# A hybrid decoder block on one core: the turned blocks of the MLP leave GpSimd's DMA queue for ScalarE's, step by step behind the weight copies

## The chip, the cores and the metric

The kernel runs on one core of a Trainium2 chip, with one launch. The metric is device time in microseconds (us) per execution. The core has five engines with instruction streams of their own: TensorE (PE, with its weight loads as PEld), VectorE (DVE), ScalarE (ACT), GpSimd (POOL) and SyncE (SP). They meet only through semaphores. DMA transfers are issued by an engine's stream and then run beside it.

## The reference

One layer on 272 tokens (16 learned tokens and 256 of the input), width 2048, all in float32:

```python
def reference(x, meta_tokens, ...):
    h = concatenate([meta, x], axis=1)
    h = h + hybrid_mixer(rmsnorm(h, norm_mix_g), w_in, ...)      # attention beside gated linear attention
    h = h + squared_relu_mlp(rmsnorm(h, norm_mlp_g), w_ff1, w_ff2)
    return rmsnorm(h, final_norm_g)[:, N_META:]

def squared_relu_mlp(xn, w1, w2):                                 # 2048 -> 8192 -> 2048
    return jnp.square(jax.nn.relu(xn @ w1)) @ w2
```

The change touches the MLP alone.

## The kernel before

**Products.** Each float32 product is made of a high and a low part. A weight block is loaded in halves of 512 KB by SP into `raw` (5 buffers, L163). ScalarE copies the high part into `w` (L165; L126 in the parts before the MLP), VectorE subtracts and leaves the low part beside it (L166), and `w` has 5 buffers as well. TensorE then multiplies high by high, high by low and low by high (L955, L956, L957).

**The MLP** has the tokens on the partitions where its blocks are wide: `token_rows` goes over 512 columns of weights in four steps (`wide_weights`), each of four k-tiles in two halves, and leaves two banks `pt` of 128 tokens by 512 columns. For the next product the result is wanted the other way about, columns on the partitions. That is what `turn` does: VectorE transposes 32 by 32 squares (L968) into one half of a tile `turn` (tag "o", 2 buffers), four transfers carry its four partition groups to a DRAM tile `there` (2 buffers, L973), and one transfer brings the whole back into the other half (L975).

`hidden` is called 14 times. It makes the squared ReLU (L983, L984, with `u` as its one buffer), turns it, and splits the turned block into `a` for the second product (L224 on ScalarE, a subtract on VectorE). `gathered` sums the second product over groups of columns in `rows`; at the last of the wide groups, four times, it turns `rows` and GpSimd adds the result to the residual `h` (L1012). `spread` runs once, ahead of the first turn: it writes the inverse norms of the 256 tokens to DRAM (`line`, L936) and reads them back to all partitions (`r2b`, L937).

**What sets the order.** `behind` is a list of work with a count; `made` is called once a weight step, after the step's second high copy on ScalarE, counts every entry down, and at zero runs it with the place behind that copy (`issue_after`). `hidden` puts its split at a count of 7. The instruction streams are otherwise placed by a scheduler that goes by its own model of time. After the MLP's wide part, eight blocks of ordinary form follow, the last sums, the final norm and the output (`finish`, L1108 and L1111). The program's closing code has line 1186, its opening code line 1182.

Besides the turns and `spread`, two transfers of the attention part are on GpSimd's queue: `fdram` (L497) and `negc` (L734).

Of the kernel before, what the change touches and what calls it, by code (L numbers as in the profile page):

```python
# [12 lines left out]
ALU = mybir.AluOpType  # L13
# [3 lines left out]
P = 128  # L17
# [3 lines left out]
NT = 256  # L21
# [44 lines left out]
def trunk(ctx: ExitStack, tc: tile.TileContext, hT, w_small, w_all, consts, w_alpha2, out):  # L66
    nc = tc.nc
    serial = [0]

    def nm(s):  # L70
        serial[0] += 1
        return f"{s}_{serial[0]}"
# [11 lines left out]
    def bank(pool, s):  # L84
        return pool.tile([P, 512], F32, tag="bank", name=nm(s))
# [46 lines left out]
    def next_weights(keep_hi=None, meta=False, low=False):  # L132
        c = chunk[0]
        chunk[0] += 1
        parts = []
        for i in range(2):
            hi, lo, step = weight_half(c, i, None if keep_hi is None else keep_hi[:, HK * i : HK * (i + 1), :], meta, low)
            copied = step(0, HK)
            parts.append((hi, lo))
        made(copied)  # L140
        return lambda k: (parts[k // HK][0][:, k % HK, :], parts[k // HK][1][:, k % HK, :])

    behind = []
# [46 lines left out]
    def gemm2(w, x, k0=0, nk=KT, pool=None):  # L190

        ps = bank(pool or pg, "ps")
        for k in range(nk):
            hi, lo = w(k0 + k)
            mac2(ps, hi, lo, x[:, k], k == 0, k == nk - 1)
        issued()
        return ps
# [16 lines left out]
    def total(ps, t=None):  # L214

        b = tmp.tile([P, NT], F32, tag="evb", name=nm("evb"), bufs=1)
        nc.scalar.copy(b, ps[:, NT:512])  # L217
        if t is None:
            t = tmp.tile([P, NT], F32, tag="evt", name=nm("evt"), bufs=4)
        nc.vector.tensor_tensor(t, ps[:, 0:NT], b, op=ALU.add)  # L220
        return t

    def split_to(dst_hi, dst_lo, src):
        nc.scalar.copy(dst_hi, src)  # L224
        nc.vector.tensor_tensor(dst_lo, src, dst_hi.bitcast(F32), op=ALU.subtract)
# [66 lines left out]
    def take(*shape):  # L292
        n = 1
        for d in shape:
            n *= d
        ap = room[:, at_room[0] : at_room[0] + n]
        at_room[0] += n
        if len(shape) == 2:
            ap = ap.rearrange("p (a b) -> p a b", b=shape[1])
        return ap  # L300
# [143 lines left out]
    both = take(NA)  # L444
# [96 lines left out]
    def gla_head(hd, sg, ready=None):  # L541
# [91 lines left out]
        for i in range(4):  # L633
            ps = gemm_all(next_weights(meta=True))
            vT = tmp.tile([P, NA], F32, tag="vT", name=nm("vT"))
            nc.vector.tensor_tensor(vT, ps[:, 0:NA], rb, op=ALU.mult)
            nc.gpsimd.tensor_copy(vg[:, NB * i : NB * (i + 1)], vT[:, 4 * C :])
            later(2 - i % 2 if hd else 1, lambda i=i, vT=vT: turn(i, vT))
# [234 lines left out]
    for j0 in range(0, KT, 2):  # L873
        gates = ahead if j0 == 0 else [gate() for _ in range(4)]
        w = next_weights()
        for j in range(2):
            t = total(gemm2(w, of, k0=8 * j, nk=8))
            nc.vector.tensor_tensor(gates[2 * j], gates[2 * j], t, op=ALU.mult)
        for j in range(2):
            t = total(gemm2(next_weights(), og))  # L880
# [11 lines left out]
    ht = h[:, :, NM:NA]  # L892
# [23 lines left out]
    r2 = gat.tile([P, 2], F32, name="r2", bufs=1)  # L916
    r2b = keep.tile([P, NT], F32, tag="rb", name="r2b")
    parts = gat.tile([P, 2 * NT + 64], F32R, name="parts", bufs=1)[:, 48 : 48 + 2 * NT]
# [14 lines left out]

    def spread():
        line = dram.tile([1, NT], F32, name="line")
        nc.gpsimd.dma_start(line.rearrange("o (t p) -> p (o t)", t=2), r2)  # L936
        nc.gpsimd.dma_start(r2b, line.to_broadcast([P, NT]))  # L937

    def relu2(a, f, ps):
        t = total(ps)  # L940
# [20 lines left out]
        issued()  # L961
        return pts

    def turn(rows):

        both = gat.tile([P, KT * P], F32, tag="o", name=nm("turn"))
        for t, r in enumerate(rows):
            nc.vector.transpose(both[:, 0:1024].rearrange("p (i t j r) -> p t i j r", i=4, t=2, r=32)[:, t],  # L968
                                r().rearrange("p (j i s) -> p i j s", i=4, s=32))
        back = both[:, 1024:]  # L970
        there = dram.tile([P, 1024], F32, tag="there", name=nm("there"), bufs=2)
        for c in range(4):
            nc.gpsimd.dma_start(there.rearrange("(i s) (c e) -> c s i e", i=4, c=4)[c],  # L973
                                both[32 * c : 32 * c + 32, 0:1024].rearrange("s (i e) -> s i e", i=4))
        nc.gpsimd.dma_start(back, there)  # L975
        return back.rearrange("p (c t j r) -> p j t c r", c=4, t=2, r=32)

    def hidden(a, b, pt):

        u = gat.tile([P, 2, 512], F32, tag="u", name=nm("u"), bufs=1)  # L980

        def part(t):
            nc.scalar.activation(u[:, t, :], pt[t], AF.Relu, scale=r2[:, t : t + 1])  # L983
            nc.scalar.activation(u[:, t, :], u[:, t, :], AF.Square)  # L984
            return u[:, t, :]

        back = turn([lambda t=t: part(t) for t in range(2)])

        def parts():
            for t in range(2):  # L990
                hi, lo = (a[:, 4 * b : 4 * b + 4, o, P * t : P * t + P].rearrange("p j (c r) -> p j c r", r=32)
                          for o in range(2))
                split_to(hi, lo, back[:, :, t])

        behind.append([7, parts])

    rows = gat.tile([P, 2, D], F32, name="rows", bufs=1)

    def gathered(g, b, pt):

        rs = [rows[:, t, 512 * b : 512 * b + 512] for t in range(2)]
        for r, ps in zip(rs, pt):
            if g == 0:
                nc.scalar.copy(r, ps)
            else:
                nc.vector.tensor_tensor(r, ps, r, op=ALU.add)
        if g < NG - 2:
            return
        back = turn([lambda r=r: r for r in rs])
        for j in range(4 * b, 4 * b + 4):  # L1010
            r = ht[:, j, :].rearrange("p (t c r) -> p t c r", t=2, r=32)
            nc.gpsimd.tensor_tensor(r, r, back[:, j - 4 * b], op=ALU.add)  # L1012

    def normed(j):
        square_sum(j, acc)
# [5 lines left out]
    for g in range(NG):  # L1021
        a = operand(keep, "a", at=48, tag="s1")
        if g == 1:
            spread()
        for b in range(2 if g == NG - 1 else 4):
            hidden(a, b, *token_rows(x2, 1, norm2 if (g, b) == (0, 0) else None))
        for b0, n in () if g == NG - 1 else ((0, 2), (2, 1), (3, 1)):
            for b, pt in enumerate(token_rows(a, n), b0):
                gathered(g, b, pt)
# [10 lines left out]
    for n in range(NL):  # L1040
        j, ps = KT - NL + n, bank(pg if n < 3 else px, "ps")
# [149 lines left out]
```

## Time and profile before

| what | value |
|---|---|
| time, median of 3 (lowest to highest) | 1534.65 us (1534.22 to 1535.03) |
| profiled execution | 1534.53 us |
| span in its trace | 1532.7 us |
| mean granted clock of TensorE | 0.997 |
| TensorE busy | 1517.7 us, 99% |
| VectorE, ScalarE, GpSimd busy | 65%, 52%, 13% |
| DMA | 311.97 MB, mean 204 GB/s |

The trace's times count from the start of the span; the profiled execution is 1.8 us longer than its span. The rows of the trace name an instruction by its line (L973), its engine, its operation, and what it writes and reads (`there<-turn`); a number behind "x" is a count. A name like POOLq is the engine's sequencer: waits, drains and issues. "[27.27 <-DVE turn L968]" says that the engine idled 27.27 us before, and which work ended that.

### The profile page before, as it was taken

What the parts mean: (1) busy time and instruction counts of PE and PEld (TensorE: products, weight loads), DVE (VectorE), ACT (ScalarE), POOL (GpSimd) and SP (SyncE); (2) the same over time, 40 slices, a digit from 0 to 9 for tenths busy, and PEclk for the clock granted to TensorE, in tenths of its full rate; (3) what the DMA queues carried; (4) which work ended last, traced back from release to release, by engine and by line L of the source; (5) the groups of instructions that cost most, each with busy time, mean ns of one, the idle gap of its engine ahead of it and who ended that gap; (6) DMA issues with size and microseconds to landing.
All of it is one profiled execution on the core that took longest, in us unless ns stands there. A gap on an engine that the chain in (4) does not pass through costs nothing.

```text
span 1532.7 us, 23498 instructions
## 1 busy us (share of the span) xinstructions
PE 1517.7 (99%) x8982; PEld 1367.8 (89%) x8982; DVE 992.4 (65%) x1421; ACT 799.0 (52%) x1203; POOL 198.3 (13%) x322
## 2 busy tenths in 40 slices
PE   9999999999999999999999999999999999999996
PEld 8999999999999999999998888888888888888996
DVE  7898858586666666666787555445555556657655
ACT  7666454555555544445666455444543554345563
POOL 6012010111100000000011110001100110430022
PEclk9999999999999999999999999999999999999998
DMA  9545555565555665566566787668866777877561
GB/s 327 169 153 173 185 160 191 159 214 168 165 169 188 196 199 196 195 200 198 189 208 195 206 268 235 201 194 258 255 199 201 226 254 225 285 235 241 196 201 65
DMA packets 172593, 311.97 MB, mean 204 GB/s; under 512 B 10601, under 2 KB 124785, under 8 KB 172353
## 3 DMA queue, kind: packets, MB, share of 16 engines
q1 hardware_dynamic: 165744, 289.62, 59.0%
q0 software_dynamic: 6304, 20.14, 4.3%
q8 instruction: 70, 1.15, 0.3%
q10 hardware_dynamic: 432, 0.72, 0.1%
q14 instruction: 43, 0.34, 0.1%
HBM read 298.89 MB, written 11.54 MB: 203 GB/s over the span
## 4 chain that ended last, share of the span: by engine, by line
PE 95%; DVE 2%; ACT 1%; issue 1%; DMA 0%; POOL 0%; SPq 0%; POOLq 0%; DVEq 0%; ACTq 0%
PE ps L179 27%; PE ps L180 14%; PE pt L957 12%; PE pt L955 12%; PE pt L956 12%; PE psa L184 4%; PE psa L188 4%; PE psa L186 4%; PE ps L397 1%; PE ps L1060 1%; PE ps L399 1%; DVE w L127 1%; PE ps L1044 1%; PE pa L595 0%; DMA raw<-w_all_dram 0%
## 5 line engine op out<-in xcount | busy, mean ns | idle before, releaser
L127 DVE TENSOR_TENSOR w<-raw,w 128x1024 fp32r<-128x1024 f32 x314 | 389.5, 1241 | 161.1 <-ACT w L126 158.2
L166 DVE TENSOR_TENSOR w<-raw,w 128x1024 fp32r<-128x1024 f32 x208 | 255.6, 1229 | 240.1 <-ACT w L165 239.9
L126 ACT CAST w<-raw 128x1024 fp32r<-128x1024 f32 x314 | 329.2, 1049 | 138.8 <-PE ps L180 78.4
L179 PE MATMUL ps<-x,w 128*128 128x512 f32 x1056 | 355.8, 382 | 0.0
L165 ACT CAST w<-raw 128x1024 fp32r<-128x1024 f32 x208 | 217.5, 1046 | 261.7 <-PE pt L957 258.3
L180 PE MATMUL ps<-x,w 128*128 128x256 f32 x1056 | 289.6, 274 | 0.0
L179 PEld LDWEIGHTS ps<-x,w 128*128 128x128 f32 x1056 | 198.2, 188 | 33.7
L180 PEld LDWEIGHTS ps<-x,w 128*128 128x128 f32 x1056 | 198.3, 188 | 0.0
L184 PE MATMUL psa<-x,w 128*128 128x272 f32 x640 | 181.8, 285 | 0.0
L188 PE MATMUL psa<-x,w 128*128 128x272 f32 x640 | 179.7, 282 | 0.0
L186 PE MATMUL psa<-x,w 128*128 128x272 f32 x624 | 176.0, 282 | 0.0
L957 PE MATMUL pt<-w,x 128*128 128x512 f32 x448 | 170.3, 380 | 0.0
L955 PE MATMUL pt<-w,x 128*128 128x512 f32 x448 | 170.3, 380 | 0.0
L956 PE MATMUL pt<-w,x 128*128 128x512 f32 x448 | 170.2, 380 | 0.0
L957 PE MATMUL pt<-w,a 128*128 128x512 f32 x384 | 145.9, 380 | 0.0
L955 PE MATMUL pt<-w,a 128*128 128x512 f32 x384 | 145.9, 380 | 0.0
L956 PE MATMUL pt<-w,a 128*128 128x512 f32 x384 | 145.9, 380 | 0.0
L184 PEld LDWEIGHTS psa<-x,w 128*128 128x128 f32 x640 | 120.2, 188 | 0.2
L188 PEld LDWEIGHTS psa<-x,w 128*128 128x128 f32 x640 | 120.2, 188 | 0.1
L186 PEld LDWEIGHTS psa<-x,w 128*128 128x128 f32 x624 | 117.4, 188 | 0.0
L217 ACT COPY evb<-ps 128x256 f32<-128x256 f32 x104 | 38.6, 371 | 126.4 <-PE ps L180 126.4
L957 PEld LDWEIGHTS pt<-w,x 128*128 128x128 f32 x448 | 84.1, 188 | 14.5
(324 smaller groups left out, 2335.1 us busy)
## 6 DMA issues: line engine op xcount, KB each, us to landing
raw<-w_all_dram SPq DMA_DIRECT2D x537, 512.0 KB, 4.5
there<-turn POOLq DMA_DIRECT2D x72, 128.0 KB, 4.7
turn<-there POOLq DMA_DIRECT2D x18, 512.0 KB, 4.8
raw<-w_all_dram SPq DMA_DIRECT2D x8, 384.0 KB, 6.6
h<-hT_dram SPq DMA_DIRECT2D x8, 275.0 KB, 7.0
negc<-fdram POOLq DMA_DIRECT2D x1, 1088.0 KB, 8.7
out_dram<-o SPq DMA_DIRECT2D x2, 512.0 KB, 2.7
raw<-w_all_dram SPq DMA_DIRECT2D x2, 256.0 KB, 3.6
```

Source lines behind the costliest of these rows:

```text
L126: copied = nc.scalar.copy(hi[:, k, :], r).ins
L127: nc.vector.tensor_tensor(lo[:, k, :], r, hi[:, k, :].bitcast(F32), op=ALU.subtract)
L165: copied = nc.scalar.copy(hi, r).ins
L166: nc.vector.tensor_tensor(lo, r, hi.bitcast(F32), op=ALU.subtract)
L179: nc.tensor.matmul(steps(ps), hi, steps(row(x)), start=first, stop=False)
L180: nc.tensor.matmul(steps(ps[:, 0:NT]), lo, steps(x[:, 0, :]), start=False, stop=last)
L184: nc.tensor.matmul(steps(ps[:, X_LO]), hi, steps(x_lo[:, k]), start=first, stop=False, skip_group_check=True)
L186: nc.tensor.matmul(steps(ps[:, 0:NA]), lo, steps(x_hi[:, k]), start=False, stop=last and hi is None, skip_group_check=True)
L188: nc.tensor.matmul(steps(ps[:, 0:NA]), hi, steps(x_hi[:, k]), start=False, stop=last, skip_group_check=True)
L955: nc.tensor.matmul(steps(ps), xh, steps(hi), start=(k == 0), stop=False)
L956: nc.tensor.matmul(steps(ps), xh, steps(lo), start=False, stop=False)
L957: nc.tensor.matmul(steps(ps), xl, steps(hi), start=False, stop=(k == KT - 1))
```

## The change

The four transfers to `there` and the one back go from GpSimd's queue to ScalarE's. They are no longer issued when the transposes are made: the four stand behind the copy of the 5th following weight step, the one back behind the 6th, and what uses the turned block (the split in `hidden`, GpSimd's adds in `gathered`) behind the 7th. `spread`'s two transfers go to SP's queue.

```diff
     def spread():
         line = dram.tile([1, NT], F32, name="line")
-        nc.gpsimd.dma_start(line.rearrange("o (t p) -> p (o t)", t=2), r2)
-        nc.gpsimd.dma_start(r2b, line.to_broadcast([P, NT]))
+        nc.sync.dma_start(line.rearrange("o (t p) -> p (o t)", t=2), r2)
+        nc.sync.dma_start(r2b, line.to_broadcast([P, NT]))
...
-    def turn(rows):
+    def turn(rows, then):
...
-        for c in range(4):
-            nc.gpsimd.dma_start(there.rearrange("(i s) (c e) -> c s i e", i=4, c=4)[c],
-                                both[32 * c : 32 * c + 32, 0:1024].rearrange("s (i e) -> s i e", i=4))
-        nc.gpsimd.dma_start(back, there)
-        return back.rearrange("p (c t j r) -> p j t c r", c=4, t=2, r=32)
+
+        def away():
+            for c in range(4):
+                nc.scalar.dma_start(there.rearrange("(i s) (c e) -> c s i e", i=4, c=4)[c],
+                                    both[32 * c : 32 * c + 32, 0:1024].rearrange("s (i e) -> s i e", i=4))
+
+        behind.append([5, away])
+        behind.append([6, lambda: nc.scalar.dma_start(back, there)])
+        behind.append([7, lambda: then(back.rearrange("p (c t j r) -> p j t c r", c=4, t=2, r=32))])
...
-        back = turn([lambda t=t: part(t) for t in range(2)])
-
-        def parts():
+        def parts(back):
...
-        behind.append([7, parts])
+        turn([lambda t=t: part(t) for t in range(2)], parts)
...
-        back = turn([lambda r=r: r for r in rs])
-        for j in range(4 * b, 4 * b + 4):
-            r = ht[:, j, :].rearrange("p (t c r) -> p t c r", t=2, r=32)
-            nc.gpsimd.tensor_tensor(r, r, back[:, j - 4 * b], op=ALU.add)
+
+        def add(back):
+            for j in range(4 * b, 4 * b + 4):
+                r = ht[:, j, :].rearrange("p (t c r) -> p t c r", t=2, r=32)
+                nc.gpsimd.tensor_tensor(r, r, back[:, j - 4 * b], op=ALU.add)
+
+        turn([lambda r=r: r for r in rs], add)
```

How the streams move. TensorE's is the same in both. The first place is ScalarE's stream behind the first turned block, from the copies of the fifth following weight step on. Before, no transfer stands in it:

```order
L165 CAST w_9740<-raw_9739 128x1024
L165 CAST w_9745<-raw_9744 128x1024
L165 CAST w_9774<-raw_9773 128x1024
L165 CAST w_9779<-raw_9778 128x1024
L983 ACTIVATE u_9723<-pt_9581,r_9245 128x512
L983 ACTIVATE u_9723<-pt_9582,r_9245 128x512
L165 CAST w_9808<-raw_9807 128x1024
L984 ACTIVATE u_9723<-u_9723 128x512 x2
L165 CAST w_9813<-raw_9812 128x1024
L224 CAST a_9252<-turn_9568 128x4x128 x2
```

After the change the same place holds the four transfers, and two copies on, the one back:

```order
L165 CAST w_9730<-raw_9729 128x1024
L165 CAST w_9735<-raw_9734 128x1024
L975 DMA there_9570<-turn_9563 32x4x256 x4
L165 CAST w_9768<-raw_9767 128x1024
L165 CAST w_9773<-raw_9772 128x1024
L979 DMA turn_9563<-there_9570 128x1024
L987 ACTIVATE u_9718<-pt_9571,r_9245 128x512
L987 ACTIVATE u_9718<-pt_9572,r_9245 128x512
L165 CAST w_9803<-raw_9802 128x1024
L988 ACTIVATE u_9718<-u_9718 128x512 x2
L165 CAST w_9808<-raw_9807 128x1024
L224 CAST a_9252<-turn_9563 128x4x128 x2
```

The copies, the activations and the split keep their order; the transfers are put between them, and the one back waits in ScalarE's stream for the four to land.

The second place is GpSimd's stream at the gathered blocks. Before, it issues the transfers of two blocks and then adds:

```order
L973 DMA there_12555<-turn_12552 32x4x256 x4
L973 DMA there_12570<-turn_12567 32x4x256 x4
L975 DMA turn_12552<-there_12555 128x1024
L975 DMA turn_12567<-there_12570 128x1024
L1012 TENSOR_TENSOR h<-h,turn_12552 128x256 x4
L1012 TENSOR_TENSOR h<-h,turn_12567 128x256 x4
```

After the change only the adds are left, of all four gathered blocks one behind the other:

```order
L1015 TENSOR_TENSOR h<-h,turn_12552 128x256 x4
L1015 TENSOR_TENSOR h<-h,turn_12558 128x256 x4
L1015 TENSOR_TENSOR h<-h,turn_12702 128x256 x4
L1015 TENSOR_TENSOR h<-h,turn_12864 128x256 x4
L901 TENSOR_TENSOR acc_9251<-acc_9251,hsq_13712 128x256
```

Every transfer of the MLP has left this stream. The third place is SP's stream where `spread` stands now, between the weight loads (`raw`):

```order
L163 DMA raw_9533<-w_all_dram 128x4x256
L936 DMA line<-r_9245 128x2x1
L163 DMA raw_9573<-w_all_dram 128x4x256
L937 DMA r2b<-line 128x256
L163 DMA raw_9578<-w_all_dram 128x4x256
```

One weight load goes between the two, and the load behind `r2b` is issued after `line` has landed.

## The prediction

> **What bounds the kernel now.** I read the page's busy shares first, then busy time by stage, then the waits, then the end of the chain.
>
> ```profile
> PE 1517.7 (99%) x8982; PEld 1367.8 (89%) x8982; DVE 992.4 (65%) x1421; ACT 799.0 (52%) x1203; POOL 198.3 (13%) x322
> ```
>
> Stretches of the program (columns: TensorE busy, its weight loads, VectorE, ScalarE, GpSimd, granted clock, DMA share, GB/s). The middle one is the MLP, where all the turns lie:
>
> ```profile
> core 0: us, PE busy (x) PEld busy (x) DVE busy (x) ACT busy (x) POOL busy (x), PEclk, DMA share, GB/s
> 0.00:860.00 860.00, 857.84 (x5734) 796.68 (x5735) 612.23 (x1006) 467.01 (x794) 112.60 (x196) 1.00 0.59 191
> 860.00:1430.00 570.00, 570.00 (x2652) 488.27 (x2651) 321.57 (x323) 279.84 (x321) 66.01 (x107) 1.00 0.74 233
> 1430.00:1533.00 103.00, 89.89 (x600) 82.89 (x598) 58.61 (x93) 52.13 (x89) 19.67 (x19) 0.96 0.46 149
> ```
>
> TensorE is busy in 570.00 of the 570.00 us that hold the turns, at a granted clock of 1.00. So a shorter turn buys nothing there. The change can lose time in this stage, by making TensorE wait, and can gain none. What is not TensorE lies in the last stretch: 103.00 − 89.89 = 13.1 us. The chain of waits ends with these two rows (start, duration, engine):
>
> ```profile
> 1517.06 2.35 POOL o L1108 x2
> 1519.41 3.12 issue
> ```
>
> What follows 1522.5 is the closing code, line 1186: a drain on each engine, then a barrier (duration in ns min/median/max, then first and last start):
>
> ```profile
> L1186 POOLq DRAIN  x3: 40/102/9402, 1522.5 to 1532.4; - x3
> L1186 DVEq DRAIN  x2: 19/936/1853, 1522.3 to 1532.2; - x2
> L1186 ACTq DRAIN  x2: 8/79/150, 1524.6 to 1532.2; - x2
> ```
>
> GpSimd's drain of 9402 ns began at 1522.5 and ended at 1531.9. Its last arithmetic was over long before, and so was everybody else's. GpSimd's last products, the transfers of the output, and SP's drains behind the waits for these transfers:
>
> ```profile
> 1522.56 1.59 POOL L1108 TENSOR_TENSOR o<-h,r_half 128x256 f32<-128x256 f32 x2 [3.15 <-DVE r_half L1093]
> L1111 SPq DMA_DIRECT2D out_dram<-o x4: 332/338/348, 1518.0 to 1524.2; - x4
> L1111 ACTq DMA_DIRECT2D out_dram<-o x3: 338/374/381, 1522.8 to 1524.2; - x3
> DMA to landing us min/median/max: 1.8/2.6/3.1
> L1186 SPq DRAIN  x2: 7/7/7, 1527.4 to 1527.5; - x2
> ```
>
> GpSimd's arithmetic ends at 1522.56 + 1.59 = 1524.15, the last output lands by about 1524.2 + 3.1 = 1527.3, and SP is done at 1527.5. From 1527.5 to 1531.9 nothing runs but GpSimd's drain, and the barrier behind it takes 1532.7 − 1531.93 = 0.77 us. VectorE's drain of 1853 ns from 1522.3 ends with its last product and is no such case. So **4.4 us of the span are GpSimd's drain alone**.
>
> **The change part by part.** GpSimd's queue loses the second and third of these kinds of transfer (count, KB each, median us to landing), and the two in `spread`:
>
> ```profile
> raw<-w_all_dram SPq DMA_DIRECT2D x537, 512.0 KB, 4.5
> there<-turn POOLq DMA_DIRECT2D x72, 128.0 KB, 4.7
> turn<-there POOLq DMA_DIRECT2D x18, 512.0 KB, 4.8
> ```
>
> It keeps two, `fdram` and `negc`: of 94 transfers 92 go.
>
> *The drain.* Two drains of GpSimd with no transfer issued since the one before take 102 and 40 ns (the row above), and the one at the kernel's start takes 186:
>
> ```profile
> L1182 POOLq DRAIN  x1: 186/186/186, 0.4 to 0.4; - x1
> ```
>
> The long one, which has all 94 transfers behind it, lasts 7.8 us beyond GpSimd's last product. SP, with 537 large loads behind it, drained in 7 ns, so the price belongs to GpSimd's queue. No trace here shows whether it grows with the number of transfers. Bounds: 0.2 us (no work on the queue) and 7.8 us (a fixed price once the queue was used). In proportion, 2 × 7.8 / 94 = 0.17 us, an estimate. I take the low end: of four drains in this run the three without transfers are short, and 2 of 94 is nearer to none. Then GpSimd is done at about 1524.4, SP at 1527.5 ends last, and the span ends at 1527.5 + 0.77 = 1528.3: **−4.4 us**. Any drain below 3.3 us gives the same, since SP covers it.
>
> *Four more issues and one back issue on ScalarE, per turn.* TensorE's pace, the copies that follow it, and the copies' and the subtracts' groups in the MLP (busy us, mean ns of one | idle before, and what ended it):
>
> ```profile
> 876.85 0.38 PE L955 MATMUL pt<-w,x 128*128 128x512 f32 x1
> 877.07 0.38 PE L956 MATMUL pt<-w,x 128*128 128x512 f32 x1
> 877.29 0.38 PE L957 MATMUL pt<-w,x 128*128 128x512 f32 x1
> 1296.81 1.05 ACT L165 CAST w<-raw 128x1024 fp32r<-128x1024 f32 x1 [1.59 <-PE pt L957]
> 1299.45 1.05 ACT L165 CAST w<-raw 128x1024 fp32r<-128x1024 f32 x1 [1.59 <-PE pt L957]
> L165 ACT CAST w<-raw 128x1024 fp32r<-128x1024 f32 x196 | 204.9, 1046 | 250.2 <-PE pt L957 247.7 <-DMA raw<-w_all_dram 2.5
> L166 DVE TENSOR_TENSOR w<-raw,w 128x1024 fp32r<-128x1024 f32 x197 | 242.2, 1229 | 234.9 <-ACT w L165 234.9
> ```
>
> A matmul starts every 0.22 us, a half block holds 12, so a buffer of `w` falls free every 2.64 us; ScalarE copies 1.05 of that and idles 1.59. Five buffers: when a copy starts, four others are ahead, 4 × 2.64 = 10.56 us; less the copy and VectorE's 1.23 us, **8.28 us of delay reach TensorE as nothing**. The four `there` issues take 4 × 0.37 = 1.5 us (ACT issues above), inside one idle of 1.59. The back transfer is queued one weight step later, and ScalarE must wait there for the four to land. With L from issue to landing, in us after the copy it hangs on: the step's two copies end at 2.64 and 5.28, the back issue goes at max(5.28, 1.5 + L). At L = 4.7 that is 6.2, 0.9 later than the queue alone would have it. Behind it stand Relu (two of 0.69), the next copies, the squares (two of 0.63) and two casts of `a` (0.61):
>
> ```profile
> L983 ACT ACTIVATE u<-pt,r 128x512 f32<-128x512 f32 x28 | 18.9, 689 | 13.1 <-PE pt L957 13.1
> L984 ACT ACTIVATE u<-u 128x512 f32<-128x512 f32 x28 | 16.1, 625 | 0.0
> L224 ACT CAST a<-turn 128x512 fp32r<-128x512 f32 x28 | 15.9, 614 | 0.0
> ```
>
> The copy behind Relu then starts at 6.2 + 0.37 + 1.35 = 7.9 in place of 6.87, 1.0 late. The casts of `a` need the back transfer: 6.2 + 4.8 = 11.0, and the copy behind them starts at about 12.3 in place of 12.15. Each later copy wins back up to 1.59. Both delays lie inside 8.28: **0 us**. Were the cover gone they would cost 1.0 and 0.15 us a turn. In general the copy is 2L − 9.5 late (both transfers taken alike); delay carries into the next turn from L = 7.1 (2L − 14.3 a turn) and a single turn stalls TensorE from 8.9. Where two blocks are gathered at once, eight transfers share `there`'s two tiles, and VectorE's subtracts queue behind a transpose that waits for GpSimd's adds: there the stall begins at L = 6.4 and is 2L − 12.8.
>
> L is not in the trace for ScalarE's queue. The bounds are the output writes above (1.8) and the slowest `there` (7.7):
>
> ```profile
> L973 POOL DMA_DIRECT2D there<-turn x72: 551/551/587, 869.6 to 1395.2; - x72
> DMA to landing us min/median/max: 2.3/4.7/7.7
> L975 POOL DMA_DIRECT2D turn<-there x18: 552/557/573, 878.9 to 1400.9; - x18
> ```
>
> I take 4.7: same bytes, same stage, same traffic of weights. SP's larger loads, at 4.5, stand on the same side.
>
> *GpSimd.* It loses 72 × 0.55 = 40 us of issuing and its place in the turn; its adds to `h` move behind the seventh weight step, and the residual that reads them comes after 1430. With TensorE busy throughout the stage, nothing there waited for it: 0.
>
> *`spread` on SP.* The weight loads queue behind `r2b`, which waits for `line`:
>
> ```profile
> 858.60 0.79 POOL L936 DMA_DIRECT2D line<-r  x1 [16.16 <-DVE r L268]
> 869.00 0.56 POOL L937 DMA_DIRECT2D r2b<-line  x1 [9.62 <-DMA line<-r]
> 872.63 1.04 ACT L165 CAST w<-raw 128x1024 fp32r<-128x1024 f32 x1 [2.45 <-DMA raw<-w_all_dram]
> L163 SPq DMA_DIRECT2D raw<-w_all_dram x4: 368/368/368, 860.9 to 868.8; - x4
> DMA to landing us min/median/max: 9.5/10.0/11.6
> L163 SPq DMA_DIRECT2D raw<-w_all_dram x4: 368/368/368, 871.5 to 879.4; - x4
> DMA to landing us min/median/max: 6.9/7.1/9.2
> ```
>
> The last rows are SP's loads between 860 and 870, then 870 and 880, one every 2.64 us. `line` lands at 858.6 + 0.8 + 9.6 = 869.0; the load behind `r2b` leaves at about 869.4 in place of 863.5, 5.9 late, and the later ones catch up. A load leaves when the copy and subtract before it have freed its buffer, and of five buffers its own copy comes some 5 × 2.64 − 2.3 = 10.9 us later; landing in 7 to 10, it makes that copy 2 to 5 us late (estimates). The slack of 8.28 is already short by the 2.45 us of the third row; 5 + 2.45 = 7.5 still fits, barely. Bounds 0 and 3 us; I take 0.
>
> **Sum.** Against the profiled execution (1534.53 us, span 1532.7): −4.4 + 0 + 0 = 1530.1. The median shown is 0.1 above that execution: **1530.2 us**. Runs of before lie within 0.4 of their median, and small stalls may take 0.6, so this case alone spans 1529.4 to 1531.2. A change of 0.2%, 3.1 us, is about what a measurement of this kernel can tell.
>
> **Rivals.**
>
> *The drain is a fixed price.* Two transfers are still on GpSimd, and the trace has no drain behind only a few. Against it: nothing of the transfers can be outstanding, the last of them (1400.9) over 100 us old; for it: a flat clean-up need not count. Then the span stays, 1534.6. So does a drain that shrinks by less than 3.1 us. The Trainium skill ("DMA: Bandwidth & Descriptors", section "Issuing engines are not separate DMA queues") speaks for this one: transfers run on the same 16 engines whoever issues them, and only issue time on the sequencer is saved. By that rule the change is worth nothing; in the trace the issues on GpSimd are indeed off the path, but the 7.8 us drain is a cost that it does not count. Together 0.38.
>
> *ScalarE's queue is held by its own waits: slower.* Place: the back issue of a turn, and above all the gathered blocks. From L = 6.4 the gathered blocks stall TensorE, from 7.1 single turns carry delay over. At L = 7.7: 2 × 7.7 − 12.8 = 2.6 us; and with 5.9 late in a first turn and 1.1 more in each further one, the fourth of a group is 9.2 late, 0.9 over the slack, in three groups: 5.4 us in all: 1534.6 + 5.4 = 1540.0, or 1535.6 with the shorter drain. At L = 10 a turn costs 5.7 us, some 80 in all. For it: 7.7 did occur. Against it: it is the slowest of 72, and writes by ScalarE's and SP's queues, those of the output, landed in 3.1 at most. The Trainium skill ("Perfetto Trace Analysis", section "DMA Instruction — HWDGE (DVE, Sync)") warns that the completion of a write to HBM can take surprisingly long; the writes to `there` are of that kind, and the median of 4.7 us against 2.6 for the output writes agrees in direction only. A stall of 3 us at `spread` belongs here only where the drain stays (1537.6; 1533.2 with the short drain). Together 0.15.
>
> **How the numbers follow.** Short drain, no stall: 0.47. Drain unchanged or nearly, or its gain eaten by a stall: 0.38. Slower: 0.15. The range from 1529.4 to 1536.5 holds the first case, the second, and stalls of up to 2 us on top of it; it leaves out the held queue's 1540 and more, some 0.13, and a few in 100 below. Faster 0.47, same 0.38, slower 0.15.
>
> **What would show it.** Right: GpSimd's last drain ends before SP's, near 1525, the span ends at about 1528.3, TensorE is still busy throughout the MLP, and ScalarE's copies wait for TensorE as now. Wrong: the same 9.4 us drain with two transfers behind it (fixed price); gaps in TensorE at the gathered blocks or next to 880, or `there` on ScalarE's queue landing after 7 us (held queue).

## The result, and the profile after

The changed kernel takes 1531.08 us (median of 13 runs, 1530.41 to 1532.01), the kernel before 1534.67 in the same comparison: a ratio of 0.9977, 95% interval 0.9968 to 0.9985. That is 3.6 us faster, against 4.4 forecast; the time is 0.9 us above the forecast and inside its range.

The closing drains of the changed kernel, line 1191 now (duration in ns min/median/max, first and last start):

```profile
L1191 POOLq DRAIN  x3: 93/188/1881, 1523.2 to 1529.7; - x3
L1191 SPq DRAIN  x3: 7/7/7, 1528.8 to 1529.1; - x3
L1191 SPq EVENT_SEMAPHORE  x9: 17/28/28, 1528.4 to 1530.0; - x9
```

GpSimd's last products in its timeline:

```profile
1523.26 1.59 POOL L1113 TENSOR_TENSOR o<-h,r_half 128x256 f32<-128x256 f32 x2 [3.15 <-DVE r_half L1098]
```

The drain of 9402 ns has become one of 1881. As before, it starts with the last products and cannot end before them: 1.881 − 1.59 = 0.29 us beyond them, where it was 9.402 − 1.59 = 7.81. Now SP, waiting for the output, is last.

TensorE's stage is untouched (busy of TensorE, its loads, VectorE, ScalarE, GpSimd, then clock, DMA share, GB/s), and so are ScalarE's copies, except for a few waits:

```profile
860.00:1430.00 570.00, 570.00 (x2652) 488.34 (x2651) 321.64 (x323) 279.22 (x321) 16.40 (x16) 1.00 0.72 232
```

```profile
ACT w L165 <- PE pt L957: 238.5, 158, 2.5
...
ACT w L165 <- DMA there<-turn: 9.8, 3, 4.2
ACT w L165 <- DMA raw<-w_all_dram: 7.7, 4, 3.4
```

The waits (us in total, times, longest) show ScalarE's weight copies held by landings for 17.5 us in all, and TensorE is still busy 570.00 of 570.00. ScalarE's splits and activations wait another 7.7 us for the turned block's transfers. The transfers that moved (lines 975 and 979 are `there` and the one back, on ScalarE's queue; line 936 is `line` on SP's):

```profile
L975 ACTq DMA_DIRECT2D there<-turn x72: 309/458/1543, 877.1 to 1405.0; - x72
DMA to landing us min/median/max: 3.7/4.3/6.3
L979 ACTq DMA_DIRECT2D turn<-there x18: 344/344/418, 884.7 to 1410.7; - x18
DMA to landing us min/median/max: 3.9/5.1/6.8
L936 SPq DMA_DIRECT2D line<-r x1: 500/500/500, 858.7 to 858.7; - x1
DMA to landing us min/median/max: 11.0/11.0/11.0
```

They land about when they did on GpSimd's queue: 4.3 after 4.7, and 5.1 after 4.8.

### The profile page after: what moved, and what is told of

Read it like the earlier page. It is cut to its first block, busy times and chain, and to the rows that moved or that the text cites. A ratio compares the mean times of both kernels' runs of the same rounds, so it can differ in the third digit from the quotient of the medians.

```text
span 1530.1 us, 23462 instructions
## 1 busy us (share of the span) xinstructions
PE 1518.0 (99%) x8982; PEld 1368.0 (89%) x8982; DVE 992.8 (65%) x1421; ACT 798.2 (52%) x1203; POOL 148.5 (10%) x230
## 3 DMA queue, kind: packets, MB, share of 16 engines
q8 instruction: 70, 1.15, 0.3%
## 4 chain that ended last, share of the span: by engine, by line
PE 94%; DVE 2%; ACT 2%; issue 1%; DMA 1%; POOL 0%; POOLq 0%; DVEq 0%; ACTq 0%
PE ps L179 26%; PE ps L180 13%; PE pt L957 12%; PE pt L956 12%; PE pt L955 12%; PE psa L184 4%; PE psa L188 4%; PE psa L186 4%; PE ps L397 1%; DVE w L127 1%; DMA raw<-w_all_dram 1%; PE ps L399 1%; PE ps L1065 1%; ACT w L126 1%; PE pa L595 0%
```

## Experiments

Theory: GpSimd's drain pays for every transfer that it issued since its last drain, some 83 ns each, and the change is worth what of that lay beyond the end of everything else. Rivals: it pays by bytes or packets; it is a fixed price; it belongs to the end of the program and not to the transfers. Apart from that: does any of the moved waits cost TensorE, and why is the gain 0.8 us short?

### The price of the drain

**e1: the number without the bytes.** The changed kernel with 90 tiny transfers added:

```diff
+        for i in range(5):
+            nc.gpsimd.dma_start(spot[len(turns) - 1, i : i + 1, :], unit[0:1, 0:64].bitcast(F32))
```

> The changed kernel with 90 transfers of 256 bytes added on GpSimd's queue, 5 to each turn, so that 92 transfers stand there again with hardly any bytes. If the closing drain pays by the number of transfers (7.8 us / 94 = 83 ns each): 92 x 83 ns = 7.6 us beyond GpSimd's last product, and the time is back at about 1534.5. If it pays by bytes or packets (20.14 MB, 6304 packets before): about 0.5 us, covered by SP, 1531.1. TensorE's stages unchanged in both.

```profile
L1198 POOLq DRAIN  x3: 40/102/9242, 1531.7 to 1541.5; - x3
```

```profile
1531.77 1.60 POOL L1120 TENSOR_TENSOR o<-h,r_half 128x256 f32<-128x256 f32 x2 [3.15 <-DVE r_half L1105]
```

```profile
q0 software_dynamic: 3056, 1.15, 0.3%
```

```profile
L971 POOL DMA_DIRECT2D spot<-unit x90: 484/484/553, 759.6 to 827.5; - x90
```

(Drains, GpSimd's last products, the page's line on GpSimd's queue with packets, MB and share, and the added transfers.) With 92 transfers and 1.15 MB the drain is back: 9.242 − 1.60 = 7.64 us, where 7.6 was expected by number and 0.5 by bytes. The added transfers need nothing from the turns, and the scheduler put all 90 between 760 and 828 us, not beside the turns: they were issued some 700 us before the closing drain, and it pays for them all the same. The time missed: 1544.95, with runs from 1534.24 to 1555.52. In the profiled run (1543.49) GpSimd's last products start 9.2 us later than before the change, so that excess arose while TensorE worked ("what was not expected" below). From there to the end of the span it is 10.0 us, as it was before (10.1).

**e2 and e3: part of the transfers.** In e2 only the transfers back are on GpSimd's queue, in e3 the first 9 of the 18 turns:

```diff
-        behind.append([6, lambda: nc.scalar.dma_start(back, there)])
+        behind.append([6, lambda: nc.gpsimd.dma_start(back, there)])
```

```diff
+        eng = nc.gpsimd if len(turns) <= 9 else nc.scalar
...
-                nc.scalar.dma_start(there.rearrange(
+                eng.dma_start(there.rearrange(
```

> The changed kernel with the 18 transfers back from DRAM alone on GpSimd's queue, 20 transfers in all with 10.5 of the 20.1 MB. By number: 20 x 83 ns = 1.7 us of drain, covered by SP's waits for the output, time as the changed kernel, 1531.1. By bytes: 4.1 us of drain, about 0.5 us past SP, 1531.6.

> The changed kernel with the first 9 of the 18 turns on GpSimd's queue, 47 transfers. By number or by bytes: 3.9 to 4.2 us of drain, some 0.3 us past SP: 1531.4. A price that does not depend on how much (all or nothing): 7.8 us, 1534.6.

Drains and last products, e2:

```profile
L1191 POOLq DRAIN  x3: 40/93/3351, 1522.1 to 1527.5; - x3
```

```profile
1522.11 1.59 POOL L1113 TENSOR_TENSOR o<-h,r_half 128x256 f32<-128x256 f32 x2 [3.15 <-DVE r_half L1098]
```

and e3:

```profile
L1196 POOLq DRAIN  x3: 40/93/5563, 1521.7 to 1527.7; - x3
```

```profile
1521.68 1.59 POOL L1118 TENSOR_TENSOR o<-h,r_half 128x256 f32<-128x256 f32 x2 [3.15 <-DVE r_half L1103]
```

1.76 us with 20 transfers, 3.97 with 47. Both carry 10.56 MB, so bytes are out: by them the two would be alike. Packets are out too: they are 2768 in e2, 3200 in e3 and 3056 in e1, which does not follow the drain. In e3 the last of the 47 was issued at 1210.0, over 300 us before the closing drain; that drain ends at 1521.7 + 5.56 = 1527.3, some 0.6 us after SP's first closing drain (1526.6). The times are 1529.85 (ratio 0.997, 0.9958 to 0.9982) and 1530.32 (0.9972, 0.996 to 0.9984), 1.1 to 1.3 us below what was expected of each; the part on the missing 0.8 us comes back to that.

**e4 and e9: the same 94 transfers, cleared up early.** The kernel before with one line more, behind the last turn:

```diff
     for f in range(8, KT):
+        if f == 12:
+            tc.keep_in_program_order(nc.gpsimd.drain())
         relu2(a, f, gemm2(next_weights(low=True), x2))
```

> The kernel before with one more drain of GpSimd behind its last turn, while TensorE still has about 100 us of work; the 94 transfers stay on GpSimd's queue. If the drain clears up what transfers left behind, the early one takes the 7.8 us unseen, the closing one is short (0.2 us past the last product), and the time falls to about that of the changed kernel, 1531.1. If the long drain belongs to the end of the program, the closing one stays at 7.8 us and the time at 1534.6.

> The kernel before with the early drain once more, in more rounds. It measured 1530.3 against 1531.1 of the changed kernel. If clearing up early is worth all that the moved transfers are worth, and the changed kernel's slightly longer tail is its own, it is again at 1530.0 to 1530.6; if the difference was scatter, at 1531.0.

The added drain, the closing ones and the last products of e4:

```profile
L1032 POOLq DRAIN  x1: 8794/8794/8794, 1401.4 to 1401.4; - x1
L1188 POOLq DRAIN  x3: 34/93/1689, 1522.7 to 1528.1; - x3
```

```profile
1522.68 1.59 POOL L1110 TENSOR_TENSOR o<-h,r_half 128x256 f32<-128x256 f32 x2 [3.15 <-DVE r_half L1095]
```

The early drain takes 8.79 us at 1401, beside TensorE's work, and leaves 0.10 for the end. The time is 1530.29 in e4 and 1530.31 in e9 (ratios 0.9973, intervals 0.9962 to 0.9983 and 0.9963 to 0.9983): the whole gain, with not one transfer moved. The drain is paid once for what came since the one before; it does not belong to the end.

**e7 and e10: under the cover.** e7 also moves `fdram` and `negc` to SP, e10 is e2 with the early drain of e4.

> The changed kernel with the last two transfers of GpSimd (fdram, negc) on SP's queue as well, so none is left. By number of transfers: the drain falls by another 0.17 us under SP's cover, time as the changed kernel, 1530.2 to 1531.1. If any use of GpSimd's queue has a price at the end, below 1530.

> The changed kernel with the 18 transfers back on GpSimd's queue and the early drain. The closing drain falls from 1.75 to 0.1 us past the last product, both under SP's waits for the output: no change against that kernel without the drain, 1529.6 to 1530.2. If the drain were still on the path at 1.75 us, 1.5 less.

e7's drain is 1691 ns, 0.10 beyond 1.59 of products. e10's closing drain is 1789 ns, 0.20 beyond, where 0.1 was expected: its early drain stands at 1389.5, and one transfer back follows at 1411.9. The times are 1530.80 (0.9976, 0.9967 to 0.9986) and 1530.20 (0.9973, 0.9962 to 0.9984, against 1529.85 without the early drain). Below some 3 us the drain costs nothing that these runs can tell: e2's 1.76 us and e10's 0.20 both end before SP's wait for the output.

In one row: beyond the last product, 0.10, 0.20, 0.29, 0.45, 1.76, 3.97, 7.64 and 7.81 us with 0, 1, 2, 4, 20, 47, 92 and 94 transfers since the last drain (the one with 4 is e6, below: a drain of 2052 ns over 1.60 of products). **0.10 us + 82 ns per transfer** gives 0.10, 0.18, 0.26, 0.43, 1.74, 3.95, 7.64 and 7.81.

These are closing drains, over 100 us behind the last transfer. The early drains are less regular. Those of e9 and e10:

```profile
L1033 POOLq DRAIN  x1: 10507/10507/10507, 1402.1 to 1402.1; - x1
L1037 POOLq DRAIN  x1: 6132/6132/6132, 1389.5 to 1389.5; - x1
```

Their records start with the issue of a transfer back, some 0.56 us. For the 94 and 19 transfers issued by then the rule gives 7.8 and 1.7 us; e4's early drain, 8.79 us, has 94 too. So a drain right behind a transfer that has not landed took longer than the rule, by 0.4 to 3.9 us beyond the issue, and what fills that time stays open.

### The waits that moved

**e6: `spread` back on GpSimd's queue.**

```diff
-        nc.sync.dma_start(line.rearrange("o (t p) -> p (o t)", t=2), r2)
-        nc.sync.dma_start(r2b, line.to_broadcast([P, NT]))
+        nc.gpsimd.dma_start(line.rearrange("o (t p) -> p (o t)", t=2), r2)
+        nc.gpsimd.dma_start(r2b, line.to_broadcast([P, NT]))
```

> The changed kernel with the two transfers of spread back on GpSimd's queue: 4 transfers, drain 0.3 us past the last product. If spread on SP costs nothing, as forecast, the time is that of the changed kernel, 1530.2 to 1531.1; if the loads held behind it cost TensorE up to 3 us, this kernel is that much faster.

1530.53 (0.9974, 0.9965 to 0.9984), half a microsecond under the changed kernel and inside the scatter of both. SP's held loads cost no more than that.

**e12: the counts of 5 and 6 taken away.**

```diff
-        behind.append([5, away])
-        behind.append([6, lambda: nc.scalar.dma_start(back, there)])
+        away()
+        nc.scalar.dma_start(back, there)
```

> The changed kernel without the counts of 5 and 6: the transfers are queued on ScalarE as soon as the scheduler sees them ready, some four weight steps earlier, the same number of issues and waits per turn. By the slack of 8.28 us nothing reaches TensorE: 1530.2 to 1531.1. If the counts are what keeps ScalarE from waiting, for the transposes above all, several us slower, 1535 or more.

1531.06 (0.9977, 0.9968 to 0.9986): the same as with the counts. Where in the five weight steps ScalarE issues the transfers does not matter to the time, though its weight copies now wait 26.2 us for the landings of `there`, in place of 9.8.

**e11 and e8: more waits in ScalarE's queue.** One and two transfers more per turn, each waiting for the one ahead:

```diff
-        behind.append([5, away])
-        behind.append([6, lambda: nc.scalar.dma_start(back, there)])
+        behind.append([5, lambda: (away(), nc.scalar.dma_start(back, there), nc.scalar.dma_start(again, back))])
```

(e8 has `nc.scalar.dma_start(more, again)` behind these. Both also queue the transfer back at the count of 5; e12 shows that its place alone costs nothing.)

> The changed kernel with one more wait per turn in ScalarE's queue: the copy of the turned block to DRAM, issued once the transfer back has landed. Two more waits cost 26 us, where the landing of there had risen to 5.5 median and 9.3 at most. With one more and landings near 5 the copies run 6 to 7 us late, inside 8.28: 1531 to 1534. If any further wait breaks the cover, 1540 to 1550.

> The changed kernel with two more waits in ScalarE's queue per turn: behind the transfer back, ScalarE also issues a copy of the turned block to DRAM and a copy of that copy, each once the one before has landed. By the forecast's slack: back issued at 5.8, the third transfer at 11.3, the fourth at 16.1, so the copies of the next weights run up to 6.9 us late; 8.28 covers that, TensorE stays busy at single turns, and only the two blocks gathered at once may cost up to 5 us: 1531 to 1536. If ScalarE's waits reach TensorE, each of 18 turns pays two waits of some 5 us less the idle of 1.59: well over 1580.

Both missed, upwards. e11 takes 1538.85 (nine runs, 1530.47 to 1540.89; a tenth took 1558.98 and is left out; ratio 1.002, 1.0008 to 1.0033), e8 1557.08 (1.0138, 1.0114 to 1.0162). What TensorE waited for (us in total, times, longest) in e8, the longest first:

```profile
PE pt L955 <- ACT a L224: 4.8, 2, 3.8
PE ps L180 <- DVE w L127: 2.7, 4, 0.8
PE pt L957 <- DVE a L225: 2.1, 3, 1.0
```

and in e11:

```profile
PE pt L957 <- DVE a L225: 2.0, 3, 0.8
```

The first thing to be late is not a weight but `a`, the turned block itself: the first gathered product of a group needs the block that the fourth `hidden` turned, and that split stands behind the held queue. In e11 TensorE waited for no weight in the MLP, so the slack of 8.28 us, worked out for weights, was not used up there. The rest of e11's and e8's loss is told below.

### The missing 0.8 us

**e5: the changed kernel once more.**

> The changed kernel once more. It measured 1531.1, 0.9 above the forecast. If the 0.7 us wait of TensorE near 1497 and the longer barrier of its trace belong to that one execution, they are gone here and the time is 1530.2 to 1530.5; if they belong to the kernel, they recur and the time is 1531.1.

1531.05 (0.9977, 0.9968 to 0.9986): it recurs. In the first trace of the changed kernel TensorE had one wait that the kernel before does not have; it ended at 1500.3, not near 1497 (us in total, times, longest):

```profile
PE ps L1049 <- DVE h L906: 0.7, 1, 0.7
```

That wait does not recur: in e5 GpSimd's last products start at 1522.69, 0.13 later than before the change. What recurs is the tail:

```profile
L1192 SPq EVENT_SEMAPHORE  x9: 17/28/28, 1527.8 to 1529.4; - x9
L1192 POOLq DRAIN  x3: 93/188/1882, 1522.7 to 1529.0; - x3
L1192 SPq DRAIN  x3: 7/7/7, 1528.2 to 1528.5; - x3
L1192 POOLq EVENT_SEMAPHORE_RANGE_CLEAR  x1: 142/142/142, 1528.6 to 1528.6; - x1
```

```profile
L1117 ACTq DMA_DIRECT2D out_dram<-o x3: 344/374/392, 1523.0 to 1524.3; - x3
DMA to landing us min/median/max: 1.8/2.6/3.4
```

The slowest output transfer lands after 3.4 us in place of 3.1, and all of SP's closing waits run one behind the other after it: SP is done at 1528.2, 0.7 later than the forecast's 1527.5. From there to the end of the span (1529.5) it is 1.3 us in place of 0.77, since GpSimd's last drain (1529.0) stands 0.3 us behind its clearing of semaphores (1528.6 + 0.14) and takes 0.19, where it took 0.04 before. Together 1.2: −4.4 + 1.2 = −3.2, the span of e5 against that of before.

From the start of GpSimd's last products to the end of the span the forecast had 1528.3 − 1522.56 = 5.7 us. It is 6.8 in both traces of the changed kernel, and 5.7 in e2, e4, e9 and e10, the faster ones, where that gap is not there. The gap is not the whole account: e12 is without it (6.3 us there) and takes as long as the changed kernel. What opens the gap and delays the landing was not found.

## Why the prediction was right

- **TensorE's stage can lose and not gain:** so it was, 570.00 of 570.00 before and after.
- **The drain is the gain:** right, in mechanism and size. But no trace showed then whether the drain shrinks with the number of transfers; the prediction chose the low end of its bounds, and e1 to e4 showed only afterwards that the choice was sound. The estimate of 83 ns per transfer, made in proportion from one row, was 82 by eight rows; 0.2 us were forecast for what remains, 0.29 came.
- **What ends last then:** right that it is SP behind the output, but mis-sized: SP at 1527.5 and a barrier of 0.77 were taken over from the trace of before. They measured 1528.2 and 1.3 in e5. That is the whole distance between −4.4 and −3.2 us.
- **ScalarE's queue:** 0 was right, L was 4.3 and 5.1 where 4.7 and 4.8 were taken; an issue took 0.46 where 0.37 was taken. But the cover named for it was not the only one: the list of who waits left out TensorE's wait for `a`, and e11 and e8 show that this comes first. The rival's prices (2L − 12.8, carry from L = 7.1) rested on the weights alone, and no run here bears them out. Its comparison of 4.7 us for `there` with 2.6 for the output says nothing of writes to DRAM, since both are such writes.
- **`spread` on SP:** 0, as forecast. `line` took 11.0 us, and ScalarE's waits for weight loads rose from 2.5 to 7.7 us, all of it inside the slack.
- **The fixed price:** ruled out by e2 and e3. The Trainium skill's rule beside it ("DMA: Bandwidth & Descriptors", "Issuing engines are not separate DMA queues") holds for the transfers themselves, whose landings hardly changed (4.3 us after 4.7, 5.1 after 4.8); but it counts only the time to issue as what another issuer can save, and here 82 ns more per transfer fell due at GpSimd's drain.

## What to carry to other kernels

Read the last microseconds of the trace. Where GpSimd's closing drain ends after every other engine is done, count the transfers that GpSimd issued: here each cost 82 ns, however small and however long landed. One early drain, in a stretch where nothing waited for GpSimd, took that away without moving a transfer. When a wait is put into a queue, list every reader of what stands behind it, the result that the wait serves included.

## What was not expected of the hardware

TensorE's pace changed for hundreds of microseconds, in e11 from a short wait on. Its timeline there:

```profile
935.27 0.38 PE L955 MATMUL pt<-w,a 128*128 128x512 f32 x1
935.49 0.39 PE L956 MATMUL pt<-w,a 128*128 128x512 f32 x1
936.35 0.50 PE L957 MATMUL pt<-w,a 128*128 128x512 f32 x1 [0.47 <-DVE a L225]
...
1000.35 0.38 PE L955 MATMUL pt<-w,a 128*128 128x512 f32 x1
1000.58 0.39 PE L956 MATMUL pt<-w,a 128*128 128x512 f32 x1
1000.80 0.38 PE L957 MATMUL pt<-w,a 128*128 128x512 f32 x1
1001.02 0.39 PE L955 MATMUL pt<-w,a 128*128 128x512 f32 x1
```

Before the wait a matmul starts every 0.220 us, after it every 0.2235, with the granted clock at 1.00 in both (TensorE's busy time and matmuls in 30 us, clock, DMA share, GB/s):

```profile
900.00:930.00 30.00, 30.00 (x139) 1.00 0.87 286
...
960.00:990.00 30.00, 30.00 (x136) 1.00 0.68 221
1200.00:1230.00 30.00, 30.00 (x136) 1.00 0.70 224
```

At 136 in place of 138 per 30 us from 936 to about 1390, some 6.6 us are lost (an estimate), beside waits of 2.0: about the distance of e11's trace to that of the changed kernel (spans of 1538.4 and 1530.1). In e8 the count falls to 133 behind its first long wait and returns to 139 after a later one. In e8 the granted clock falls as well, around its wait of 3.8 us for `a`:

```profile
930.00:960.00 30.00, 25.77 (x102) 0.89 0.80 267
960.00:990.00 30.00, 30.00 (x133) 1.00 0.73 230
```

In e1 the count falls from 93 to 91 per 20 us at about 898, with no wait of TensorE in the rows and 70 us after the last added transfer was issued, and stays low to 1460: 1.5 to 2% of that time, 9 us or so (an estimate). So a wait is not what it takes. This could be behind the wide scatter of e1 and e11, of which one execution each was profiled; what sets the pace was not tried. In e8 the waits (11 us), the pace and the lower clock account for most but not all of the 26 us.
